# Attention on one core: rows of Q, K and V dealt to the partitions four in a row

## The chip, the cores and the metric

The kernel runs on one core of a Trainium2 chip. The metric is device time in microseconds of one execution, the median of three runs of the plain program. A profiled execution gives the trace; its times are those that the views below show. Engines are called by the profile's names: PE (TensorE, the matrix engine) and PEld (its weight loads), DVE (VectorE), ACT (ScalarE), POOL (GpSimd) and SP (SyncE, which here only issues transfers). Transfers run on 16 DMA engines that all queues share.

## The reference

```python
def setup_inputs():
    batch = 8
    seq_len = 2048
    d_model = 512
    # q, k, v: float32 [batch, seq_len, d_model]

def reference(q, k, v):
    d_k = q.shape[-1]
    scores = np.matmul(q, k.transpose(0, 2, 1)) / np.sqrt(d_k)
    attn_weights = special.softmax(scores, axis=-1).astype(np.float32)
    return np.matmul(attn_weights, v)
```

Eight independent attentions of 2048 queries on 2048 keys, without a mask. For one query the order of the keys doesn't matter, as long as K and V have the same one, and each query's output depends on no other query.

## The kernel before, in words

**Tiles.** A batch of K, Q or V is four chunks of 512 rows; a chunk is four tiles of 128 rows. With the old layout, row `p` of tile `n` stands on partition `p`, so a partition holds rows `p`, `128 + p`, `256 + p` and `384 + p` of the chunk (`srcs`, "(n p) d -> p n d"). All is computed in float16 with sums in float32.

**Loads.** `load` (line 118) brings a chunk of Q or K, 1 MB of float32, in one transfer of POOL's queue that casts to float16 on the way into a staging tile; there are three staging tiles (`stage`). `load_v` (line 207) brings a chunk of V straight into `vraw`, one of two buffers for a batch. In `vraw` two rows of V lie side by side, each with a gap of eight elements behind it (`VP = D + 8`); the gap behind the second one holds a 1, which makes the matmul sum the weights of the softmax as a 257th column. `dma_transpose` (line 143), on SP's queue, turns a staged chunk into `kops[c][0]` (`kraw`) or `qraw`, with the 512 dimensions on partitions, and frees the staging tile. `store` (line 405), on SP's queue too, writes a finished tile of 128 queries by 512 to memory. The output tiles come from a pool of seven (`opool`).

**Products.** Both products are done as two-by-two blocks with seven products in place of eight. For the scores, `Group` takes a pair of key tiles and 1024 queries (`sp`), for which DVE forms sums of blocks of K (`k_sums`, lines 181 to 184) and of Q (`q_sums`, lines 198 to 201); its matmuls stand on line 291. The exponential (line 227) leaves the weights in `left` and `right`, keys on partitions. For the output, `Pair` takes one tile of 128 queries from each half of the 1024 and all keys; DVE forms sums of the weights (`p_sums`, lines 340 to 343) and of V (`v_sums`, lines 215 to 218); its matmuls stand on line 386, with V's blocks as the moving operand of 256 or 257 columns. ACT and DVE scale and combine the results (lines 395, 398, 418 to 447), and `store` sends them off.

**Order.** The order of all work is written out by hand. The main loop runs over 32 steps `g`, four for a batch, each with 28 slots of score products of the coming 1024 queries between the output products of the present ones. `PLAN` says in which slot the next batch's chunks are loaded and transposed; `KSUMS`, `VSUMS` and `sums_of` say when DVE forms the sums. A load waits on POOL's queue for a free staging tile (that is, for an earlier transpose) or for the V buffer of two batches ago.

**The opening.** The first chunks of Q and K come row tile by row tile as float32, in eight transfers of 256 KB on the queues of SP and ACT (`load_first`, line 128), and are cast by DVE and ACT (`round_first`, line 132). Once the first tile of K has landed, POOL issues the other loads of batch 0 in the order `LOADS = 'q1 k1 q2 k2 k3 v0 v1 q3 v2 v3'`, `q1` in two pieces of two tiles; some land in `right` and `left` of the second set of weight tiles, which are not in use yet (`SPARE`), so the profile shows them as `right<-in_k_dram` and the like. PE itself transposes the chunks of Q and K of batch 0 (line 153), except `q2`, which SP's queue transposes. Then POOL waits twice, on lines 694 and 695, until that transpose and the last chunk of V have landed, before it issues loads for batch 1. Until the first rows are there, PE runs matmuls on zeros (`idle`, line 657).

Of the kernel before, what the change touches and what calls it, by code (L numbers as in the profile page):

```python
# [12 lines left out]
def kernel(  # L13
# [21 lines left out]
    nc = tc.nc  # L35
    P = 128
    B, T, D = q.shape
    F16 = mybir.dt.float16
# [11 lines left out]
    NT = QH // P  # L50
    NQT = 2 * NSP
    NJ = NKB // 2
    CH = 4
    NCH = NKB // CH
    H = D // 2
    VP = D + 8
    TP = H + 8
    NG = NJ // 2
    NE = 6
# [3 lines left out]
    const = ctx.enter_context(tc.tile_pool(name="const", bufs=1))  # L63
# [12 lines left out]
    def bank(name):  # L76
        t = psum[name].tile([P, 512], F32, tag=name)
        return t
# [10 lines left out]
    for c in range(NCH):  # L89
# [3 lines left out]
    qraw = [const.tile([P, 2 * NT, ND, P], F16, name=f"qraw{n}") for n in range(2)]  # L93
    qsum = [const.tile([P, NT, 2, P], F16, name=f"qs{n}") for n in (1, 2, 4)]

    vraw = [const.tile([P, NJ, 2, VP], F16, name=f"vh{n}") for n in range(2)]
    vt1 = const.tile([P, NJ, TP], F16, name="vt1")
    vt2 = const.tile([P, NJ, H], F16, name="vt2")
    vt4 = const.tile([P, NJ, H], F16, name="vt4")
# [1 line left out]
    pts = {}  # L101

    srcs = {
        "k": k.rearrange("b (n p) d -> b p n d", p=P),
        "q": q.rearrange("b (n p) d -> b p n d", p=P),
        "v": v.rearrange("b (n p) d -> b p n d", p=P),
    }

    def load(what, b, c, pieces=(CH,), room=None):
        t = staged.get((what, b, c))  # L110
        if room is not None:
            t = staged[what, b, c] = room
        if t is None:
            t = staged[what, b, c] = stage.tile([P, CH, D], F16, tag="stage", name="stage")
        n = CH - sum(pieces)
        for w in pieces:
            at = c * CH + n
            nc.gpsimd.dma_start(out=t[:, n:n + w, :], in_=srcs[what][b, :, at:at + w, :])
            n += w

    firsts = {}
# [1 line left out]
    def load_first(what, n, queue, room):  # L123

        if (what, 0, 0) not in staged:
            staged[what, 0, 0] = stage.tile([P, CH, D], F16, tag="stage", name="stage")
        firsts[what, n] = room
        queue.dma_start(out=room, in_=srcs[what][0, :, n, :])

    def round_first(what, n):  # L130
        f = nc.vector.tensor_copy if what == "q" else nc.scalar.copy
# [8 lines left out]
    def dma_transpose(what, b, c):  # L140
        src = staged.pop((what, b, c))
        dst = raw_of(what, b, c)
        nc.sync.dma_start_transpose(
            out=dst[:, 0:CH].rearrange("p n c r -> p (n c) r"),
            in_=src[:].rearrange("p n d -> p (n d)"),
        )
# [30 lines left out]
    def k_sums(c):  # L177
        a11, a12, a21, a22 = k_blocks(c)
        _, s1, s2, s4 = kops[c]
        return [  # L180
            lambda: add(s1[:], a21, a22),
            lambda: sub(a21, a11, a21),
            lambda: sub(s2[:], s1[:], a11),  # L183
            lambda: sub(s4[:], a12, s2[:]),
        ]
# [16 lines left out]
        ]  # L202

    def load_v(b, c):
        dst = vraw[b % 2][:].rearrange("p j s d -> p (j s) d")
        ns = slice(c * CH, (c + 1) * CH)
        nc.gpsimd.dma_start(out=dst[:, ns, 0:D], in_=srcs["v"][b, :, ns, :])

    def v_sums(b, c):
        vh = vraw[b % 2]  # L210
        js = slice(c * CH // 2, (c + 1) * CH // 2)
        b11, b12 = vh[:, js, 0, 0:H], vh[:, js, 0, H:D]
        b21, b22 = vh[:, js, 1, 0:H], vh[:, js, 1, H:D]
        return [
            lambda: sub(vt1[:, js, 0:H], b12, b11),
            lambda: sub(vt2[:, js], b22, vt1[:, js, 0:H]),
            lambda: sub(b12, b22, b12),
            lambda: sub(vt4[:, js], b21, vt2[:, js]),
        ]
# [39 lines left out]
    class Group:  # L259
# [6 lines left out]
        def product(self, n):  # L266
            c, j = divmod(self.j, 2)
            a11, a12, a21, a22 = k_blocks(c)
            b11, b12, b21, b22 = q_blocks(self.sp)
            _, s1, s2, s4 = kops[c]  # L270
            t1, t2, t4 = qsum
            t3 = t3_of(self.sp)
            if n == 1:
                if self.sp not in pts:
                    new_p(self.sp)
                self.left, self.right = pts[self.sp]
                self.x = bank("qx")
# [12 lines left out]
            for dc in range(2):  # L290
                nc.tensor.matmul(  # L291
                    dst[:], lhs[:, j, dc, :], rhs[:, :, dc, :],
                    start=(n in (1, 5) and dc == 0), stop=(dc == 1),
                    skip_group_check=True,
                )
            getattr(self, f"after{n}", lambda: None)()
# [49 lines left out]
    def columns(g, which):  # L346
        i = g % 2 * 2 + "ab".index(which)
        return slice(i * P, (i + 1) * P)

    class Pair:  # L350
# [6 lines left out]
        def product(self, n, j0=0, j1=NJ):  # L357
            g = self.g
            left, right = pts[g // 2]
            s1, s2, s4 = psums.get((g, self.which), (None,) * 3)  # L360
            vh, t1, t2, t4 = vraw[g // NQT % 2], vt1, vt2, vt4
            cols = columns(g, self.which)
            alone = g >= NP - 2 and self.which == "b"
            own = "q" if alone else "p"
            self.apart = g == NP - 1
            if n == 1 and j0 == 0:
                self.x = bank("px")
            elif n == 2:
                self.y = bank(own + "y")
            elif n == 5:  # L370
                self.z = bank(own + "z")
            lhs, rhs, dst = {
                1: (lambda j: left[0][:, j, cols], lambda j: vh[:, j, 0, 0:H], "x"),
                2: (lambda j: left[1][:, j, cols], lambda j: vh[:, j, 1, 0:H], "y"),
                3: (lambda j: s4[:, j, :], lambda j: vh[:, j, 1, H:D + 1], "z"),
                4: (lambda j: right[:, j, 1, cols], lambda j: t4[:, j, :], "x"),
                5: (lambda j: s1[:, j, :], lambda j: t1[:, j, 0:H + 1], "z"),
                6: (lambda j: s2[:, j, :], lambda j: t2[:, j, :], "x"),
                7: (lambda j: right[:, j, 0, cols], lambda j: vh[:, j, 0, H:D], "x"),
            }[n]  # L380
# [20 lines left out]

        def store(self, o, half, ds=slice(0, D), queue=nc.sync):
            b, sp = divmod(self.g // 2, NSP)
            n = (2 * sp + half) * NT + self.g % 2 * 2 + "ab".index(self.which)
            queue.dma_start(out=out[b, n * P:(n + 1) * P, ds], in_=o[:, ds])

        def store_first(self, ds):
            if self.apart:
# [88 lines left out]
    def prefetch(g, slot):  # L497
        b, qt = divmod(g, NQT)
        if (g, slot) == (0, 12):
            nc.gpsimd.memset(vraw[1][:, :, 1, D:D + 1], 1.0)  # L500
# [98 lines left out]
    nc.gpsimd.memset(vraw[0][:, :, 1, D:D + 1], 1.0)  # L599

    def row():
        t = opool.tile([P, D], F32, tag="o", name="first")
# [13 lines left out]
    gate = const.tile([P, 1], F32)  # L616
# [10 lines left out]
    for n, word in enumerate(LOADS.split()):  # L627
        what, c = word[0], int(word[1])
# [63 lines left out]
    dma_transpose("q", 0, 2)  # L692

    nc.gpsimd.tensor_copy(out=gate[:], in_=qraw[1][:, NT - 1, ND - 1, 0:1])
    nc.gpsimd.tensor_copy(out=gate[:], in_=vraw[0][:, NJ - 1, 1, D - 1:D])

    braid = []
    for n, (j, own, edges) in enumerate(FIRST_GROUPS):
# [75 lines left out]
```

## Time and profile before

| | |
|---|---|
| median of three runs | 802.04 us (801.6 to 802.36) |
| profiled execution | 800.94 us, of which the span in the trace is 799.2 us |
| granted TensorE clock | 1.00 |
| instructions | 14,622 |
| DMA packets | 188,870, with 115.80 MB written |
| HBM | 100.70 MB read, 33.55 MB written |

The span runs from the first to the last instruction in the trace. A packet is one run of bytes that a DMA engine moves; sizes are those written, so a load that casts from float32 to float16 reads twice as much. `q0` is POOL's queue, `q1` is SP's. The busy share of DMA engines can be over 100%, since packets of one engine overlap. In a list of groups the columns are line, engine, operation, output and inputs, size and count, then busy time and the mean of one. The groups of transfers (KB as written, median time from issue to landing):

```profile
out_dram<-o SPq DMA_DIRECT2D x124, 256.0 KB, 3.5
vh<-in_v_dram POOLq DMA_DIRECT2D x32, 512.0 KB, 10.5
stage<-in_k_dram POOLq DMA_DIRECT2D x29, 512.0 KB, 8.0
stage<-in_q_dram POOLq DMA_DIRECT2D x28, 512.0 KB, 7.9
right<-in_k_dram POOLq DMA_DIRECT2D x2, 512.0 KB, 13.2
...
right<-in_q_dram POOLq DMA_DIRECT2D x2, 256.0 KB, 5.3
right<-in_q_dram POOLq DMA_DIRECT2D x1, 512.0 KB, 10.4
left<-in_q_dram POOLq DMA_DIRECT2D x1, 512.0 KB, 22.8
qraw<-stage SPq DMA_TRANSPOSE x28, 6.3
kraw<-stage SPq DMA_TRANSPOSE x28, 7.2
```

These times hold the waiting in the queue: the ten loads of the opening are issued within ten microseconds and land over thirty.

### The profile page before, as it was taken

What the parts mean: (1) busy time and instruction counts of PE and PEld (TensorE: products, weight loads), DVE (VectorE), ACT (ScalarE), POOL (GpSimd) and SP (SyncE); (2) the same over time, 40 slices, a digit from 0 to 9 for tenths busy, and PEclk for the clock granted to TensorE, in tenths of its full rate; (3) what the DMA queues carried; (4) which work ended last, traced back from release to release, by engine and by line L of the source; (5) the groups of instructions that cost most, each with busy time, mean ns of one, the idle gap of its engine ahead of it and who ended that gap; (6) DMA issues with size and microseconds to landing.
All of it is one profiled execution on the core that took longest, in us unless ns stands there. A gap on an engine that the chain in (4) does not pass through costs nothing.

```text
span 799.2 us, 14622 instructions
## 1 busy us (share of the span) xinstructions
PE 793.7 (99%) x5556; PEld 538.1 (67%) x5556; DVE 557.6 (70%) x1230; ACT 572.0 (72%) x1020; POOL 71.5 (9%) x105
## 2 busy tenths in 40 slices
PE   9999999999999999999999999999999999999998
PEld 6566666666666666666666666666666666666677
DVE  5786767857677676866768667686776857678564
ACT  4877777777777767777777777777677777776752
POOL 4011110001101010010100110001110011000000
PEclk9999999999999999999999999999999999999999
DMA  9999992899828999399994999849993598711112
GB/s 222 175 176 177 207 172 73 156 183 196 166 60 156 182 197 145 80 161 178 177 158 78 173 177 186 128 93 155 203 217 86 96 205 160 162 40 41 44 52 104
DMA packets 188870, 115.80 MB, mean 145 GB/s; under 512 B 122496, under 2 KB 171904, under 8 KB 188800
## 3 DMA queue, kind: packets, MB, share of 16 engines
q0 software_dynamic: 49648, 49.29, 42.9%
q1 hardware_dynamic: 138576, 65.16, 38.3%
q8 instruction: 43, 0.70, 0.4%
q10 hardware_dynamic: 576, 0.43, 0.2%
q14 instruction: 27, 0.22, 0.1%
HBM read 100.70 MB, written 33.55 MB: 168 GB/s over the span
## 4 chain that ended last, share of the span: by engine, by line
PE 99%; DMA 0%; DVE 0%; ACT 0%; issue 0%
PE t L386 49%; PE t L291 46%; PE t L234 1%; PE t L250 1%; PE tr L153 1%; DMA first<-in_q_dram 0%; PE t L657 0%; DVE kraw L156 0%; ACT o L395 0%; DVE stage L132 0%; DVE o L447 0%
## 5 line engine op out<-in xcount | busy, mean ns | idle before, releaser
L291 PE MATMUL t<-qraw,kraw 128*128 128x512 f16 x732 | 198.1, 379 | 0.0
L395 ACT ACTIVATE o<-t,r 128x256 f32<-128x256 f32 (+1 forms) x256 | 121.1, 473 | 100.5 <-DVE r L418 69.5
L386 PEld LDWEIGHTS <-s 128*128 128x128 f16 x1536 | 150.3, 98 | 56.5
L227 ACT ACTIVATE left<-t 128x512 f16<-128x512 f32 x256 | 154.1, 603 | 37.0 <-PE t L291 30.8
L398 DVE SCALAR_TENSOR_TENSOR o<-t,r,o 128x256 f32<-128x256 f32 x192 | 92.4, 482 | 102.1 <-PE t L386 60.9
L291 PEld LDWEIGHTS <-kraw 128*128 128x128 f16 x984 | 96.2, 98 | 64.2 <-issue 0.3
L291 PE MATMUL t<-qs,ks 128*128 128x512 f16 x492 | 136.5, 379 | 0.0
L386 PE MATMUL t<-vh,left 128*128 128x256 f16 x1024 | 133.0, 273 | 0.0
L386 PE MATMUL t<-vt,s 128*128 128x257 f16 (+1 forms) x1024 | 133.0, 273 | 0.0
L227 ACT ACTIVATE right<-cz 128x1024 f16<-128x1024 f32 x123 | 130.5, 1061 | 1.1 <-DVE cz L311 1.1
L386 PEld LDWEIGHTS <-left 128*128 128x128 f16 x1024 | 100.2, 98 | 37.6
L386 PEld LDWEIGHTS <-right 128*128 128x128 f16 x1024 | 100.2, 98 | 37.5 <-issue 0.4
L305 ACT COPY cz<-t 128x512 f32<-128x512 f32 x122 | 71.4, 585 | 72.8 <-PE t L291 72.4
L311 DVE TENSOR_TENSOR cz<-t,cz 128x512 f32<-128x512 f32 x123 | 84.5, 687 | 52.8 <-PE t L291 52.7
L314 DVE TENSOR_TENSOR cz<-t,cz 128x512 f32<-128x512 f32 x123 | 84.9, 690 | 43.0 <-PE t L291 41.6
L291 PEld LDWEIGHTS <-ks 128*128 128x128 f16 x738 | 72.1, 98 | 48.3 <-DVE ks L183 0.3
L291 PE MATMUL t<-qraw,ks 128*128 128x512 f16 x246 | 73.2, 379 | 0.0
L291 PE MATMUL t<-qs,kraw 128*128 128x512 f16 x246 | 73.2, 379 | 0.0
L301 ACT COPY t<-t 128x512 f32<-128x512 f32 x121 | 69.0, 570 | 4.0 <-PE t L291 0.8
L308 ACT COPY cz<-t 128x512 f32<-128x512 f32 x123 | 71.5, 581 | 0.0
L386 PE MATMUL t<-vh,s 128*128 128x257 f16 x512 | 66.7, 273 | 0.0
L386 PE MATMUL t<-vh,right 128*128 128x256 f16 x512 | 66.2, 273 | 0.1
(62 smaller groups left out, 574.0 us busy)
## 6 DMA issues: line engine op xcount, KB each, us to landing
out_dram<-o SPq DMA_DIRECT2D x124, 256.0 KB, 3.5
vh<-in_v_dram POOLq DMA_DIRECT2D x32, 512.0 KB, 10.5
stage<-in_k_dram POOLq DMA_DIRECT2D x29, 512.0 KB, 8.0
stage<-in_q_dram POOLq DMA_DIRECT2D x28, 512.0 KB, 7.9
right<-in_k_dram POOLq DMA_DIRECT2D x2, 512.0 KB, 13.2
out_dram<-o SPq DMA_DIRECT2D x6, 128.0 KB, 1.7
first<-in_q_dram SPq DMA_DIRECT2D x2, 256.0 KB, 3.3
cz<-in_q_dram SPq DMA_DIRECT2D x2, 256.0 KB, 4.8
```

Of the source, the lines that this page charges most:

```text
L153: nc.tensor.transpose(tr[:, m, dc, :], src[:, n + m, dc * P:(dc + 1) * P], ident[:])
L227: nc.scalar.activation(out=out_, in_=in_, func=EXP, scale=inv_sqrt_d)
L234: nc.tensor.matmul(st[:], kops[c][0][:, n, dc, :], qraw[0][:, half * NT:(half + 1) * NT, dc, :], start=(dc == 0), stop=(dc == ND - 1),)
L291: nc.tensor.matmul(dst[:], lhs[:, j, dc, :], rhs[:, :, dc, :], start=(n in (1, 5) and dc == 0), stop=(dc == 1), skip_group_check=True,)
L301: self.edges[0](out=self.y[:], in_=self.x[:])
L305: self.edges[1](out=self.cz[:, 1, :], in_=self.z[:])
L308: nc.scalar.copy(out=self.cz[:, 0, :], in_=self.x[:])
L311: nc.vector.tensor_add(self.cz[:, 1, :], self.x[:], self.cz[:, 1, :])
L314: nc.vector.tensor_add(self.cz[:, 0, :], self.z[:], self.cz[:, 0, :])
L386: nc.tensor.matmul(dst[:, 0:width], lhs(j), rhs(j), start=(first and j == 0), stop=(j == NJ - 1), skip_group_check=True,)
L395: nc.scalar.activation(out=out_, in_=src, func=COPY, scale=r[:])
L398: nc.vector.scalar_tensor_tensor(out=out_, in0=src, scalar=r[:], in1=out_, op0=MULT, op1=ADD)
```

## The change

Within a chunk of 512 rows, partition `p` now holds rows `4p` to `4p + 3` ("(c p n) d -> c p (n d)"). What was tile `n` of a chunk, rows `128 n + p`, is now rows `4p + n`. Q, K and V have the same dealing, so the weights and the products are the same up to the order of keys and queries, and `store` writes tile `n` of a chunk to rows `4p + n`.

For the transfers: a chunk of Q or K is one run of 8 KB in memory for each partition instead of four of 2 KB. A chunk of V is two runs of 4 KB: in `vraw` the two rows of a pair now stand without a gap, and the 1 and its gap stand behind both, so each pair has 2 x 512 + 8 elements where it had 2 x 520. The two pieces of `q1` have one run of 4 KB each for a partition. The first eight row tiles and the stores still move runs of 2 KB, now 8 KB apart in memory; the pieces of the last stores move 512 or 1024 bytes, 8 KB apart. No instruction is added or taken out.

```diff
-    VP = D + 8
...
-    vraw = [const.tile([P, NJ, 2, VP], F16, name=f"vh{n}") for n in range(2)]
+    vraw = [const.tile([P, NJ, 2 * D + 8], F16, name=f"vh{n}") for n in range(2)]
...
     srcs = {
-        "k": k.rearrange("b (n p) d -> b p n d", p=P),
-        "q": q.rearrange("b (n p) d -> b p n d", p=P),
-        "v": v.rearrange("b (n p) d -> b p n d", p=P),
+        what: x.rearrange("b (c p n) d -> b c p (n d)", p=P, n=CH)
+        for what, x in (("k", k), ("q", q), ("v", v))
     }
+    outs = out.rearrange("b (c p n) d -> b c n p d", p=P, n=CH)
+
+    def flat(t):
+        return t[:].rearrange("p n d -> p (n d)")
...
         for w in pieces:
-            at = c * CH + n
-            nc.gpsimd.dma_start(out=t[:, n:n + w, :], in_=srcs[what][b, :, at:at + w, :])
+            nc.gpsimd.dma_start(
+                out=flat(t)[:, n * D:(n + w) * D],
+                in_=srcs[what][b, c, :, n * D:(n + w) * D],
+            )
             n += w
...
-        queue.dma_start(out=room, in_=srcs[what][0, :, n, :])
+        queue.dma_start(out=room, in_=srcs[what][0, 0, :, n * D:(n + 1) * D])
...
     def load_v(b, c):
-        dst = vraw[b % 2][:].rearrange("p j s d -> p (j s) d")
-        ns = slice(c * CH, (c + 1) * CH)
-        nc.gpsimd.dma_start(out=dst[:, ns, 0:D], in_=srcs["v"][b, :, ns, :])
+        js = slice(c * CH // 2, (c + 1) * CH // 2)
+        nc.gpsimd.dma_start(
+            out=vraw[b % 2][:, js, 0:2 * D],
+            in_=srcs["v"][b, c].rearrange("p (j e) -> p j e", e=2 * D),
+        )
...
-        b11, b12 = vh[:, js, 0, 0:H], vh[:, js, 0, H:D]
-        b21, b22 = vh[:, js, 1, 0:H], vh[:, js, 1, H:D]
+        b11, b12, b21, b22 = (vh[:, js, n * H:(n + 1) * H] for n in range(4))
...
-                3: (lambda j: s4[:, j, :], lambda j: vh[:, j, 1, H:D + 1], "z"),
+                3: (lambda j: s4[:, j, :], lambda j: vh[:, j, D + H:2 * D + 1], "z"),
...
-            n = (2 * sp + half) * NT + self.g % 2 * 2 + "ab".index(self.which)
-            queue.dma_start(out=out[b, n * P:(n + 1) * P, ds], in_=o[:, ds])
+            n = self.g % 2 * 2 + "ab".index(self.which)
+            queue.dma_start(out=outs[b, 2 * sp + half, n, :, ds], in_=o[:, ds])
```

The other changed lines give the same elements of V under their new addresses: products 1, 2 and 7 in `Pair`, the two memsets of the 1, and the gate on line 695.

More of the change, by code (lines that the diff above doesn't have):

```diff
@@ L372, in product @@
             lhs, rhs, dst = {
-                1: (lambda j: left[0][:, j, cols], lambda j: vh[:, j, 0, 0:H], "x"),
-                2: (lambda j: left[1][:, j, cols], lambda j: vh[:, j, 1, 0:H], "y"),
-                3: (lambda j: s4[:, j, :], lambda j: vh[:, j, 1, H:D + 1], "z"),
+                1: (lambda j: left[0][:, j, cols], lambda j: vh[:, j, 0:H], "x"),
+                2: (lambda j: left[1][:, j, cols], lambda j: vh[:, j, D:D + H], "y"),
+                3: (lambda j: s4[:, j, :], lambda j: vh[:, j, D + H:2 * D + 1], "z"),
                 4: (lambda j: right[:, j, 1, cols], lambda j: t4[:, j, :], "x"),
@@ L378, in product @@
                 6: (lambda j: s2[:, j, :], lambda j: t2[:, j, :], "x"),
-                7: (lambda j: right[:, j, 0, cols], lambda j: vh[:, j, 0, H:D], "x"),
+                7: (lambda j: right[:, j, 0, cols], lambda j: vh[:, j, H:D], "x"),
             }[n]
@@ L499, in prefetch @@
         if (g, slot) == (0, 12):
-            nc.gpsimd.memset(vraw[1][:, :, 1, D:D + 1], 1.0)
+            nc.gpsimd.memset(vraw[1][:, :, 2 * D:2 * D + 1], 1.0)
         for kind, what, c in PLAN.get((qt, slot), ()):
@@ L598 @@
     nc.gpsimd.memset(vt1[:, :, H:H + 1], 1.0)
-    nc.gpsimd.memset(vraw[0][:, :, 1, D:D + 1], 1.0)
+    nc.gpsimd.memset(vraw[0][:, :, 2 * D:2 * D + 1], 1.0)
     def row():
@@ L694 @@
     nc.gpsimd.tensor_copy(out=gate[:], in_=qraw[1][:, NT - 1, ND - 1, 0:1])
-    nc.gpsimd.tensor_copy(out=gate[:], in_=vraw[0][:, NJ - 1, 1, D - 1:D])
+    nc.gpsimd.tensor_copy(out=gate[:], in_=vraw[0][:, NJ - 1, 2 * D - 1:2 * D])
     braid = []
```

## The prediction

> **What bounds the kernel now.** I read the page first: busy time by engine, the queues, the chain of work that ended last.
>
> ```profile
> PE 793.7 (99%) x5556; PEld 538.1 (67%) x5556; DVE 557.6 (70%) x1230; ACT 572.0 (72%) x1020; POOL 71.5 (9%) x105
> ...
> q0 software_dynamic: 49648, 49.29, 42.9%
> q1 hardware_dynamic: 138576, 65.16, 38.3%
> ...
> PE 99%; DMA 0%; DVE 0%; ACT 0%; issue 0%
> ```
>
> TensorE is busy for all but 5.5 us of the span and owns 99% of the chain. The DMA engines are also busy for 81% of the time (42.9 + 38.3), yet no transfer holds more than the very first link of the chain (the first row of Q, 0.4%). A busy PE may still be a slow PE, so the next view is the windows: matmuls in equal stretches, in the columns PE, PEld, DVE, ACT, POOL, granted clock, DMA share, GB/s.
>
> ```profile
> 100.00:200.00 100.00, 100.00 (x692) 67.54 (x690) 71.31 (x158) 73.27 (x131) 9.11 (x13) 1.00 0.91 157
> 200.00:300.00 100.00, 100.00 (x692) 67.69 (x691) 70.88 (x157) 73.07 (x132) 9.99 (x14) 1.00 0.81 152
> 700.00:760.00 60.00, 60.00 (x415) 40.38 (x413) 41.80 (x93) 44.07 (x79) 0.00 (x0) 1.00 0.12 45
> 780.00:799.20 19.20, 15.58 (x142) 13.65 (x140) 9.15 (x22) 4.99 (x11) 0.00 (x0) 1.00 0.27 97
> ```
>
> The pace is 6.92 matmuls per us at a DMA share of 0.91, 6.92 at 0.81, and 415/60 = 6.92 again where all loads are over and the share is 0.12. So traffic on the DMA engines does not slow a matmul, and lighter traffic will not speed one up. What a load can do is come too late. The only place where PE lives close to its loads is the opening, so I asked who waited there, between 9 and 42 us (total, times, longest). PE itself waits for nobody; its weight loads do:
>
> ```profile
> PEld L250 <- DVE qraw L156: 0.4, 1, 0.4
> PEld L291 <- DVE ks L183: 0.3, 1, 0.3
> PEld L234 <- DVE kraw L156: 0.2, 1, 0.2
> PEld L153 <- DMA right<-in_k_dram: 0.2, 1, 0.2
> ```
>
> Four short waits, and they run ahead of the matmuls that they feed. One is for a load: chunk 2 of K, issued at 8.24 us, takes 12.2 us to land, that is until 20.4, and its transposes on PE begin at 20.49. So loads are just in time here: they can lose, they have nothing to win.
>
> **The change, part by part.** Instruction by instruction nothing moves. The order on PE, ACT, DVE, SP and POOL is the same in both programs, and so are the waits, but for one sum on DVE at about 60 us that names a further semaphore, of the first Q load, long landed. What changes is the shape of three kinds of transfer.
>
> (1) *The loads of POOL's queue, 1 MB of float32 each, cast on the way.* A chunk was 512 runs of 2 KB and becomes 128 runs of 8 KB (Q, K) or 256 of 4 KB (V). Two windows of the DMA view give the price of a packet before (packets, MB written, share of 16 engines): 16.5 to 21.5 us, where this queue is alone, and 22 to 29 us, where a transpose runs beside it.
>
> ```profile
> q0 software_dynamic: 1038, 1.03, 124.2%
> ...
> q0 software_dynamic: 1095, 1.09, 91.3%
> q1 hardware_dynamic: 1084, 0.28, 29.6%
> ```
>
> Alone, one engine starts a packet every 5 us x 16 / 1038 = 77 ns, and each takes 1.242 x 77 = 96 ns, so neighbours overlap. A chunk of 512 packets is 32 per engine, 2.47 us. No row shows an 8 KB cast packet, so bounds: if bytes set the pace it takes 4 x 77 = 308 ns and the chunk stays at 2.47 us; if the fixed part of a packet is saved (96 - 77 = 19 ns as the largest guess, three times in four) 251 ns and 2.0 us; if wide packets no longer overlap, 4 x 96 = 383 ns and 3.06 us. I take 2.47: the queue already reads 2 x 206 = 412 GB/s there, steadily, which looks like a limit in bytes. Earlier landings are worth 0 us, since PE's pace from 9 to 780 us has no gap that a load ends. Cover: the next landing in line is always ahead of its use, by 0.1 us (K chunk 2) to some 15 us (later batches). Without that cover every microsecond of lateness in the opening is a microsecond of PE.
>
> (2) *Sharing with SP's queue.* In the second window the queues alternate packet for packet: 1095 to 1084. A pair costs 7 us x 16 / 1090 = 103 ns, so a 256-byte packet of a transpose costs about 26 ns beside a load; alone, at 58 us, 562 of them in 0.5 us, 14 ns. With packets four times as long SP's transposes and stores get fewer turns while a load runs, and all of them once it has ended. The opening is again the tight place: the transpose of Q chunk 2 (2048 packets, 128 per engine) starts at about 21.5 us, with five loads still queued.
>
> ```profile
> 36.79 0.25 POOL L694 CAST gate<-qraw 128x1 f32<-128x1 f16 x1 [20.97 <-DMA qraw<-right]
> ...
> 37.64 0.69 DVE L198 TENSOR_TENSOR qs<-qraw 128x1024 f16<-128x1024 f16 x1
> ```
>
> It lands just before 36.79, where POOL's gate sees it; the first sum that reads it begins at 37.64. After: five loads are 5 x 2.47 = 12.4 us and, with V's four at 16 packets per engine and Q's at 8, 72 turns for the transpose, 72 x 26 ns = 1.9 us; the other 56 packets follow alone in 56 x 14 ns = 0.8 us. 21.5 + 12.4 + 1.9 + 0.8 = 36.6 us: about as before. The work is the same and something always has the engines; only the order changes. Cost 0 us.
>
> Later batches have more room. The first chunk of K for batch 1 is transposed from 58.06 us and first read at 75.38, 17.3 us later, while such transposes land in 4.3 to 12.6 us:
>
> ```profile
> 58.06 2.19 SPq L143 DMA_TRANSPOSE kraw<-stage  x1
> ...
> 75.38 0.42 DVE L181 TENSOR_TENSOR ks<-kraw 128x512 f16<-128x512 f16 x1
> ...
> DMA to landing us min/median/max: 4.3/7.2/12.6
> ```
>
> A store (8 packets per engine) beside a load may land 8 x (308 - 77) ns = 1.9 us later; behind it stands a pool of seven output tiles, four of which are used up in some 24 us. 0 us.
>
> (3) *The first eight rows and all stores: 2 KB runs as before, now 8 KB apart in memory.* Alone the row loads start a packet every 83 ns (270 of them in the 1.4 us from 6.0). No row shows what the distance does. Bounds: nothing, or as dear as the worst stretch of POOL's queue, 8.2 to 8.9 us, 16 x 0.7 us / 125 = 90 ns. That is 16 packets x 7 ns = 0.1 us for the first rows of Q and K, which stand on the chain; below nothing by the same 0.1. The last stores, 1.6 us to landing, have two to four packets per engine: under 0.1 us. I take 0.
>
> (4) *V without the gap between its two rows, and the ones moved behind both.* The same matmuls of 256 or 257 columns and the same sums on other addresses. The first row of each pair (`vh` with `right`) and the second (`vh` with `s`) start at different offsets today and both take 273 ns on the page. 0 us.
>
> Sum: 0. The profiled execution has a span of 799.2 us in 800.94; the three plain runs have a median of 802.04. I forecast 799.2 and 802.0. The forecast's own range, from the bounds in (3) and a microsecond of slip in (2), is 801.2 to 803.4.
>
> **The rivals.**
>
> *Wide packets lose their overlap (slower).* Place: POOL's queue in the opening. For it: today 24% of a packet's time is hidden behind its neighbour, and nothing shows that an 8 KB cast is split as finely. Against it: bytes, not packets, look like the limit. Price: 0.6 us per load. K chunk 2 is the fourth load, 2.4 us late against a margin of 0.1; Q chunk 3 is the eighth, 4.8 us late against 0.6 (it lands at 34.1, its transposes load at 34.73). PE is stopped for 4.2 us in all: 806.2. It decides as soon as a chunk takes over about 2.7 us.
>
> *Transposes starved (slower).* For it: the alternation one for one. Against it: the sum in (2). If SP's queue gets even less than its turn, the transpose of Q chunk 2 ends only after V's last chunk, for which POOL's second gate opens at 39.7, plus 0.8: 40.5 where 37.64 is due, and DVE has 0.3 us of idle time from there to 42.5. PE would lose some 2.5 us: 804.5. The Trainium skill, in "DMA: Bandwidth & Descriptors", section "Queues, rings and completion order", says that each engine goes round the queues that have work and changes only between packets; the counts 1095 and 1084 agree. Taken alone that rule speaks against this change, as the queue with the wider packets gets the larger share; by it the time would be anything between my forecast and this rival's 804.5.
>
> *The runs stay short.* If descriptors are cut back to 2 KB, everything lands as before: 802.0, with some 49,600 packets on the queue of POOL.
>
> *Faster.* It would need matmuls that run faster with less descriptor traffic: 1 ns each is 5.6 us, 796.5. The three windows above speak against it. Earlier loads alone cannot do it: the idle time of PE is 5.5 us, of which some 3.6 lie after the last matmul.
>
> **How the numbers follow.** Forecast 0.60 and short runs 0.04 (both no change), lost overlap 0.14, starved transposes 0.10, faster 0.07, and 0.05 for a slip at the first rows or the stores that is larger than its bounds. About 0.2%, 1.6 us, is what can be told from no change here. So faster 0.07, same 0.64, slower 0.29. The predicted time is the forecast's, 802.0. The range goes up to 806.3, to take in both slower rivals, and down to 800.6; it leaves out about 0.13.
>
> **What would show it.** POOL's queue falls from 49,648 packets to about 18,000 (61 x 128 + 256 for Q and K, 32 x 256 for V, and the 1,520 small ones that 94 x 512 leaves of today's count). Its share of the engines stays near 40%. Matmuls stay at 692 per 100 us, and between 9 and 42 us PE's weight loads wait no longer than now. The gate on Q chunk 2 opens within a microsecond of 36.8, the transposes of K stay under 14 us to landing. The forecast is wrong if PE shows idle time in the opening (lost overlap: behind loads of K or Q; starved transposes: behind DVE's sum on Q), or if the pace of the matmuls moves at all.

## The result: 1.9 us slower, and the profile after

| | before | after |
|---|---|---|
| median of 11 runs each, same chip | 802.07 us (800.6 to 802.82) | 803.94 us (802.11 to 804.89) |
| ratio, 95% interval | | 1.0023 [1.0014, 1.0033] |
| profiled execution | 800.94 us, span 799.2 us | 804.89 us, span 803.1 us |

The change costs 1.9 us. The profiled execution after is the longest of its 11 runs and the one before is near the short end of its own, so the two profiles lie 3.9 us apart (803.1 - 799.2): the traces show the loss enlarged. A second profile of the changed kernel has a span of 802.5 us.

The page of the changed kernel, the lines that answer to those shown of before:

```profile
PE 795.7 (99%) x5556; PEld 539.3 (67%) x5556; DVE 557.2 (69%) x1230; ACT 572.5 (71%) x1020; POOL 58.4 (7%) x105
...
q1 hardware_dynamic: 138576, 65.16, 39.1%
q0 software_dynamic: 17776, 49.29, 38.7%
...
PE 94%; DMA 5%; DVE 0%; ACT 0%; POOL 0%; issue 0%; ACTq 0%; DVEq 0%
```

POOL's queue went from 49,648 to 17,776 packets, so the runs did become long. (The trace counts 14,623 instructions against 14,622: one semaphore instruction on DVE is new, all others are the same in number.) The chain of work is the new thing: DMA held none of it to speak of, now it holds 5%. The windows of the changed kernel (PE, PEld, DVE, ACT, POOL, granted clock, DMA share, GB/s) tell where this is not:

```profile
100.00:200.00 100.00, 100.00 (x693) 67.46 (x691) 70.39 (x155) 73.39 (x132) 7.13 (x12) 1.00 0.91 149
200.00:300.00 100.00, 100.00 (x692) 67.58 (x691) 71.15 (x158) 73.14 (x132) 7.12 (x12) 1.00 0.82 156
700.00:760.00 60.00, 60.00 (x416) 40.59 (x415) 41.72 (x92) 43.90 (x79) 0.00 (x0) 1.00 0.12 45
```

The pace is the same 692 matmuls per 100 us. The loss is older than 100 us. The chain in order of time, cut to the first 50 us of the changed kernel (start, us, what), gives its place:

```profile
1.12 5.37 DMA first<-in_k_dram
...
6.54 0.19 POOL gate L622
...
8.39 11.29 DMA right<-in_q_dram
...
19.69 21.68 DMA qraw<-right
...
41.46 0.70 DVE qs L202
```

Read it downwards: the first row of K lands at 6.49 us and opens POOL's gate; POOL issues the load of Q chunk 2, which lands at 19.68; SP's queue transposes it, until 41.37; then DVE forms the sum on it. PE has no part in the chain up to there. The same steps before, in the timeline of POOL and of SP's queue (start, us, instruction, in brackets what it waited for):

```profile
5.12 0.18 POOL L617 COPY gate<-first 128x1 f32<-128x1 f32 x1 [4.22 <-DMA first<-in_k_dram]
...
17.92 7.06 SPq L143 DMA_TRANSPOSE qraw<-right  x1
```

So the gate opens 1.4 us later, the transpose is issued 1.8 us later (19.69 against 17.92), and it is 2.9 us longer in flight, as the DMA views of before and then of the changed kernel have it:

```profile
qraw<-right SPq DMA_TRANSPOSE x1, 18.7
...
qraw<-right SPq DMA_TRANSPOSE x1, 21.7
```

It lands 4.7 us later. Before, POOL's gate saw it at 36.79 and DVE's sum on it began at 37.64, so it had some 0.8 us to spare. Now the sum begins at 41.46, 3.8 us later, and the spans lie 3.9 us apart.

PE falls behind in the opening in another way too, which this chain hides. The view by tile shows it in the first full tiles, `qraw` by `kraw` on 128 x 512 (shortest, median and longest in ns, first and last in us), before and then after:

```profile
L234 PE MATMUL t<-qraw,kraw x48: 379/379/389, 17.2 to 38.6; 128*128 128x512 f16 x48
```

```profile
L239 PE MATMUL t<-qraw,kraw x48: 379/379/389, 20.0 to 41.5; 128*128 128x512 f16 x48
```

2.8 us are gone before 20 us. 1.5 of them are lost by the first product of Q and K (9.19 us against 7.67), in waits of PE for DVE's casts of the first rows, as DVE itself waits for the DMA. The other 1.3 go by while PE's clock is still low, of which more below: from 9 to 13 us PE is busy all the time in both profiles, with 52 matmuls before and 39 after.

### The profile page after: what moved, and what is told of

Read it like the earlier page. It is cut to its first block, busy times and chain, and to the rows that moved or that the text cites. A ratio compares the mean times of both kernels' runs of the same rounds, so it can differ in the third digit from the quotient of the medians.

```text
span 803.1 us, 14623 instructions
## 1 busy us (share of the span) xinstructions
PE 795.7 (99%) x5556; PEld 539.3 (67%) x5556; DVE 557.2 (69%) x1230; ACT 572.5 (71%) x1020; POOL 58.4 (7%) x105
## 3 DMA queue, kind: packets, MB, share of 16 engines
q0 software_dynamic: 17776, 49.29, 38.7%
## 4 chain that ended last, share of the span: by engine, by line
PE 94%; DMA 5%; DVE 0%; ACT 0%; POOL 0%; issue 0%; ACTq 0%; DVEq 0%
PE t L391 49%; PE t L296 45%; DMA qraw<-right 3%; DMA right<-in_q_dram 1%; DMA first<-in_k_dram 1%; POOL right L119 0%; ACT right L232 0%; ACT o L400 0%; DVE qs L202 0%; DVE cz L316 0%; DVE qraw L204 0%; POOL stage L119 0%; ACT left L232 0%; ACT cz L313 0%; DVE vt L221 0%
## 5 line engine op out<-in xcount | busy, mean ns | idle before, releaser
L391 PE MATMUL t<-vt,right 128*128 128x256 f16 x512 | 66.3, 273 | 0.0
```

The source lines that it names most:

```text
L391: nc.tensor.matmul(dst[:, 0:width], lhs(j), rhs(j), start=(first and j == 0), stop=(j == NJ - 1), skip_group_check=True,)
```

## Two things that can end last in the opening

Set side by side, the profiles of all kernels follow one reading. Let *start* be the first matmul of those tiles and *gate* the moment when POOL's gate on Q chunk 2 opens, just after its transpose has landed. Before has start 17.2 and span 799.2, so what follows a start takes 782.0 us; the changed kernel has gate 41.51 and span 803.1, so what follows a late gate takes 761.6. The span should be the larger of start + 782.0 and gate + 761.6. The other rows were not used for the two constants. Times in us; the edits are told in the next section. The ratio and its interval are worked out over all runs and are not the quotient of two medians: for rows_new the ratio means 1.7 us where the medians differ by 1.1.

| kernel | start | gate | start + 782.0 | gate + 761.6 | span | median of runs | ratio to before, same chip |
|---|---|---|---|---|---|---|---|
| before | 17.2 | 36.79 | **799.2** | 798.4 | 799.2 | 802.07 | |
| after | 20.0 | 41.51 | 802.0 | **803.1** | 803.1 | 803.94 | 1.0023 [1.0014, 1.0033] |
| again | 19.8 | 40.92 | 801.8 | **802.5** | 802.5 | 803.75 | 1.0028 [1.0018, 1.0039] |
| late_wide | 18.1 | 36.99 | **800.1** | 798.6 | 800.1 | 801.61 | 1.0003 [0.9994, 1.0012] |
| rows_new | 18.2 | 38.18 | **800.2** | 799.8 | 800.3 | 802.55 | 1.0021 [1.0012, 1.003] |
| rows_new2 | 18.3 | 38.53 | **800.3** | 800.1 | 800.8 | 802.69 | 1.0024 [1.0015, 1.0032] |
| open_wide | 17.7 | 41.25 | 799.7 | **802.9** | 802.6 | 803.66 | 1.0028 [1.0017, 1.0039] |
| open_held | 18.1 | 36.18 | **800.1** | 797.8 | 801.5 | 802.40 | 1.0019 [1.001, 1.0028] |
| rows_old | 18.2 | 40.40 | 800.2 | **802.0** | 802.1 | 804.94 | 1.0049 [1.0035, 1.0062] |
| rows_old2 | 16.9 | 39.73 | 798.9 | **801.3** | 801.4 | 805.59 | 1.0053 [1.0038, 1.0069] |
| held | 19.4 | 34.50 | **801.4** | 796.1 | 801.6 | 803.66 | 1.0029 [1.0019, 1.0039] |
| fixed | 17.1 | 33.30 | **799.1** | 794.9 | 799.5 | 802.67 | 1.0024 [1.0005, 1.0043] |
| dummies | 18.5 | 40.11 | 800.5 | **801.7** | 801.7 | 804.11 | 1.0034 [1.0022, 1.0047] |
| split | 17.6 | 39.46 | 799.6 | **801.1** | 801.2 | 804.26 | 1.0032 [1.002, 1.0044] |
| two_rows | 18.0 | 39.40 | 800.0 | **801.0** | 801.0 | 802.92 | 1.0021 [1.0012, 1.003] |
| warm | 17.0 | 36.65 | **799.0** | 798.3 | 799.0 | 801.11 | 1.0001 [0.9993, 1.001] |
| rows_new_warm | 21.8 | 40.87 | **803.8** | 802.5 | 804.9 | 802.42 | 1.0018 [1.0009, 1.0028] |

Of the 15 rows that set no constant, 13 come within 0.5 us. The two others, open_held (+1.4) and rows_new_warm (+1.1), have a third wait that their traces name (below).

The chain that the profile traces bears this choice out in most rows, not in all. It runs through the transpose in after, open_wide, rows_old, rows_old2 and dummies, as the sums say. In again, split and two_rows, where the gate's sum is also the larger, it runs along PE from the first rows until 41 or 42 us and then over DVE. In these three DVE's sum on Q chunk 2 waits 0.6 to 1.4 us for the transpose, and DVE has no gap for 5 us from there; that the late transpose sets their end through this backlog is argued from the timeline and not shown by the chain. In rows_new, rows_new2 and rows_new_warm the chain runs through POOL's gate on the first row of K and a load of K behind it.

What the wide packets do to the transpose shows most directly in its time in flight, from issue to landing. It is 18.6 to 19.1 us in the six kernels whose opening has no wide packet (before, warm, late_wide, rows_new, rows_new2, rows_new_warm), 20.7 to 22.9 in the eight that have some, and 15.5 to 18.5 in the three that have some but hold V's last chunks back (held, fixed, open_held).

The reading of the table was made after the runs, not forecast. It holds for single executions: a start also depends on when the clock of PE rises, which differs from one execution to the next, so medians are compared only with their intervals.

It explains why the parts of the loss do not add. Two delays run side by side, and mending one uncovers the other.

## The experiments

All variants compute the same as the reference; what differs is which rows a partition holds, and when a load is issued.

**rows_new and rows_new2: the long distance alone.** The kernel before, with the new dealing for chunk 0 of batch 0 only. Its rows lie 8 KB apart; no load of Q or K gets longer runs.

```diff
+    def dealt(b, c):
+        return (b, c) == (0, 0)
...
-        queue.dma_start(out=room, in_=srcs[what][0, :, n, :])
+        src = news[what][0, 0, :, n, :] if dealt(0, 0) else srcs[what][0, :, n, :]
+        queue.dma_start(out=room, in_=src)
```

> The kernel before, with the new dealing for chunk 0 of batch 0 alone: its eight first row loads (and V's chunk 0, and that chunk's stores) read 2 KB runs 8 KB apart; every other transfer as before, no packet is wider. Theory A (the late first rows and the clock that rises later): the first row of Q lands at 4.2 to 4.6 us instead of 3.7, K's at 6.0 to 6.6 instead of 5.1, TensorE's clock rises after 9 us instead of at 7.1, and the time is 1.0 to 2.0 us over before (803.1 to 804.1). Theory B (the wide packets of POOL's queue starve SP's transposes): no difference, 802.1. Theory C (wide packets in later batches): 802.1.

Measured: 802.55 against 801.43 us, slower by 1.1; with the interval, by 1.0 to 2.4. The clock rose at 4.5 us and not after 9. The same kernel a second time:

> The kernel before with the new dealing for chunk 0 of batch 0 alone, repeated as the partner of the next: 0.8 to 2.0 us over before.

Measured: 802.69 against 801.03, slower by 1.7. The transposes of PE in the timeline of the first of these runs:

```profile
4.81 0.40 PE L166 MATMUL tr<-ident,stage 128*128 128x128 f16 x4 [0.88 <-DVE stage L145]
...
7.11 0.40 PE L166 MATMUL tr<-ident,stage 128*128 128x128 f16 x4 [1.47 <-DVE stage L145]
```

They begin at 4.23 and 5.69 us before. Here PE waits 0.88 and 1.47 us for casts whose rows have landed late. The chain of the same run, cut to its first steps (start, us, what), goes another way, over the first row of K and the load of K's chunk 1 that stands behind POOL's gate on that row:

```profile
1.13 5.07 DMA first<-in_k_dram
...
6.26 0.18 POOL gate L634
...
7.90 8.45 DMA stage<-in_k_dram
...
16.39 1.07 PE tr L166 x16
```

Before, that gate opened at 5.12 us. So the late rows are felt in two places: by PE, and by all loads that POOL issues behind the gate. The queues between 2 and 5 us (packets, MB, share of 16 engines), of before and then of the changed kernel, show the transfers themselves:

```profile
q1 hardware_dynamic: 395, 0.73, 65.2%
q10 hardware_dynamic: 244, 0.28, 26.2%
```

```profile
q1 hardware_dynamic: 198, 0.37, 45.2%
q10 hardware_dynamic: 182, 0.22, 43.5%
```

On SP's queue half as many packets move in the same 3 us, and each takes longer: 3 x 16 x 0.452 / 198 = 110 ns against 3 x 16 x 0.652 / 395 = 79 (ACT's queue, q10, holds other small packets too). rows_new has 199 packets at a share of 48.9% there, as the changed kernel. That the distance of the rows costs a microsecond or more is shown (V's chunk 0 and the stores of that chunk are dealt anew here too, but no wait of PE names them). Why, is not.

**late_wide: wide runs from batch 1 on.** The kernel before with `return b > 0` in the lines above.

> The kernel before, with the new dealing from batch 1 on (Q and K in runs of 8 KB, V still in runs of 2 KB because its gaps are kept; stores 8 KB apart); the opening is the one of before. Theories A and B: nothing on TensorE's path changes, 802.1. Theory C: most of the loss, 803.5 to 804.

Measured: 801.61 against 801.43, no difference, with an interval from 0.5 us under to 1.0 us over. So no cost of the wide runs of Q and K, nor of the stores, is seen behind the opening; V's wide runs are not in this kernel. Nor do 8 KB runs win anything later, though a chunk of K now takes 6.3 us from issue to landing instead of 8.0 (medians).

**rows_old and rows_old2: wide runs, rows in time.** The changed kernel with chunk 0 of batch 0 dealt as before, in its loads and stores (V's chunk 0 in two transfers).

```diff
-        queue.dma_start(out=room, in_=srcs[what][0, 0, :, n * D:(n + 1) * D])
+        queue.dma_start(out=room, in_=olds[what][0, 0, n])
```

> The changed kernel, with the old dealing for chunk 0 of batch 0 alone (V's chunk 0 then comes in two transfers of 256 KB); all other loads keep the wide runs. Theory A: the first rows land as before (3.7 and 5.1 us), the clock rises at about 7, and most of the loss is gone: 802.1 to 802.9, the rest being the wait for the transpose of Q chunk 2. Theory B: the transpose of Q chunk 2 still lands 3 us or more after it is due and the time stays at 803.5 to 804. Theory C: 803.9.

Measured: 804.94 against 801.43, slower by 3.5, so worse than the change itself and than any of the three theories gave.

> The changed kernel with the old dealing for chunk 0 of batch 0, repeated beside the changed kernel. Theories A and B together: the transpose still lands at about 40 us and sets the time, so undoing the rows alone gains nothing: within 0.8 us of the changed kernel, with a longer wait of DVE (1.5 us or more). If the rows were the whole loss: 1.5 us or more below it. If splitting V's chunk 0 into two transfers is what made this kernel slow: over 1 us above it.

Measured: 805.59 against 801.57, over 802.91 to 810.5. That is 1.8 us above the changed kernel on the same chip (next run), the outcome that pointed to the split of V's chunk 0. The rows land as before, the start is back at 16.9, and the end is set by the transpose: its gate opens at 39.73, and DVE waits 2.3 us for it. That the rows were a cost, and not the only one, agrees with the table. The runs up to 810.5 do not: none of these was caught in a profile.

**again:** the changed kernel once more, for a second profile.

> The changed kernel once more, for a second profile and for times on the same chip as the next three. Theory A (late first rows) and theory B (wide packets hold up the transpose of Q chunk 2), now taken together: both delays push the same chain, the rows at its start and the transpose at about 41 us, so they overlap and do not add up. 1.5 to 3 us over before; the transpose lands between 39.5 and 41.5 us and DVE's first sum on Q chunk 2 waits 0.5 to 1.5 us for it.

Measured: 803.75 against 801.57. The gate opens at 40.92, and DVE's sum waits 0.6 us for the transpose. The chain that ends last is another one than in the first profile: it runs from the first rows of Q along PE until 42.15 us and then over DVE. So in this execution the two delays nearly coincide (801.8 and 802.5 in the table).

**dummies:** the changed kernel with three more matmuls on zeros at each of two waits for rows.

```diff
-    idle(5)
+    idle(8)
...
-    idle(2)
+    idle(5)
```

> The changed kernel with three more matmuls on zeros before the first transposes (eight for five) and three more before the second ones (five for two), which fill the waits for the first rows of Q. Theory A with the clock as a part of the loss: the clock rises before 9 us instead of at 12.5, and the time falls by 0.6 to 1.3 us against the changed kernel, to 802.6 to 803.3, although the rows land as late as they do there. If the lateness alone counts and not the clock: 803.9 or up to 0.5 more.

Measured: 804.11 against 801.43, no gain, as for lateness alone. In its profile the clock rose at 7.2 us instead of 12.5, and the start came at 18.5 instead of 20.0; but the gate at 40.11 ends last, so that an earlier PE is worth nothing here.

**held: the transpose helped, rows late.** The changed kernel with V's chunks 2 and 3 issued only behind the gate on Q chunk 2, so that fewer loads share the engines with its transpose.

```diff
         if what == "v":
-            load_v(0, c)
+            if c < 2:
+                load_v(0, c)
...
+    for c in (2, 3):
+        load_v(0, c)
```

> The changed kernel with V's chunks 2 and 3 of batch 0 issued behind POOL's wait for the transpose of Q chunk 2 instead of ahead of it, so that fewer wide packets stand beside the transpose. Theory B: the transpose lands before 37 us, DVE's wait for it and the gaps on TensorE between 41 and 48 us are gone, and the time falls by 0.8 to 1.7 us against the changed kernel; what is left over before (0.8 to 2 us) is the first rows. If the transpose were not what TensorE waits for: no change.

Measured: 803.66 against 801.57; the median did not move from that of *again*, where a fall of 0.8 us or more was expected. Its gate, in the timeline:

```profile
34.50 0.18 POOL L700 CAST gate<-qraw 128x1 f32<-128x1 f16 x1 [22.09 <-DMA qraw<-right]
```

The transpose is 6.4 us earlier than in *again* and off the path, and PE is busy for 9.99 of the 10 us from 40, against 9.47 after. But the start at 19.4 is left, and 782.0 behind it is 801.4. The edit did to the transpose what it should, and the other delay took its place.

**fixed: both at once** (held and rows_old).

> Both: the old dealing for chunk 0 of batch 0, and V's chunks 2 and 3 behind POOL's wait; all other loads wide. Theories A and B together: both parts of the loss are gone, within 0.6 us of before. If there is a third part (V's chunk 0 in two transfers, stores 8 KB apart, wide packets in later batches): 1 us or more over before.

Measured: 802.67 against 801.57, so 1.1 us over before: not within 0.6, but what was expected if there is a third part. The profiled execution has start 17.1 and a span of 799.5, as before the change, and 800.46 is its shortest run; but its runs reach 810.38. So both delays can be undone together, as single executions show, and something that no profile caught keeps the median up. The median is 2.9 us under that of rows_old2, where holding V back moved nothing when the rows were late, as the larger of two delays would have it; but the intervals of these two kernels (0.4 to 3.4 and 3.0 to 5.5 us over before) overlap. The scatter stays.

**split: is it V's chunk 0 in two transfers that scatters?** The changed kernel with that alone.

> The changed kernel with V's chunk 0 of batch 0 in two transfers of one pair each (runs of 4 KB, new dealing), nothing else. It asks why the kernels with the old dealing for chunk 0 scatter from 803 to 810 us. Theory S (the split, which shifts the later loads of POOL's queue and what they wait for): this kernel scatters too, and its median is over 805. Theory E (wide packets that start early, beside rows that come in time): it stays with the changed kernel, 803.3 to 804.3, no run over 805.5.

Measured: 804.26 against 801.4, over 802.98 to 805.34 in five runs. Neither the median over 805 nor the scatter came, so nothing speaks for the split. Five runs do not rule it out: the five of rows_old, which has the split, lie just as close (803.89 to 805.79).

**two_rows: a smaller distance.** Chunk 0 of batch 0 dealt two rows to a partition: 4 KB apart.

> The changed kernel with chunk 0 of batch 0 dealt two rows in a row: its row loads read 2 KB runs 4 KB apart, V's chunk 0 stays one transfer with runs of 4 KB, all else is wide. If the distance of the first rows costs by the stretch of memory that they touch: the first rows of Q and K land between those of before and of the changed kernel (3.7 to 4.4 and 5.1 to 6.2 us), and the time lies 0.5 to 1 us under the changed kernel. If only contiguous rows are quick: as the changed kernel. Theory S expects no scatter here, theory E some (up to 806).

Measured: 802.92 against 801.4, which is neither outcome as told. The first two rows land as before (casts at 3.76 and 5.28 us), yet the third row of Q is late: cast at 8.72, before at 7.53. The delay moved one step on and did not go away; start 18.0.

**open_wide: wide runs of Q and K in the opening alone.** The kernel before with `return b == 0 and c > 0`.

> The kernel before, with the new dealing for chunks 1 to 3 of batch 0 alone: Q and K of the opening in runs of 8 KB, V still in runs of 2 KB, chunk 0 and all later batches as before; no transfer is split. If wide packets of Q and K hold up the transpose of Q chunk 2: it lands after 38 us, DVE waits, 0.5 us or more over before. If it is V's packets that do it, or the split: within 0.4 us of before. Theory E: scatter and 2 us or more over before.

Measured: 803.66 against 801.4, slower by 2.3, with all first rows in time. The waits between 33 and 50 us (total, times, longest):

```profile
DVE qs L211 <- DMA qraw<-right: 2.8, 1, 2.8
...
DVE vt L229 <- DMA vh<-in_v_dram: 1.6, 1, 1.6
...
PE t L305 <- DVE cz L328: 1.0, 1, 1.0
PE t L305 <- DMA qraw<-right: 0.9, 1, 0.9
```

DVE's sum on Q chunk 2 waits 2.8 us for the transpose, and PE stands behind it. Wide packets of Q and K alone produce the late transpose, which is 22.9 us in flight instead of 18.7; V's need not be wide. The 12 runs lie between 801.40 and 805.71, so the scatter of theory E is there too, though not up to 810.

**open_held:** open_wide with V's chunks 2 and 3 held back.

> The kernel before with the wide runs of Q and K in the opening (as in the run with wide packets in the opening alone), and V's chunks 2 and 3 of batch 0 behind POOL's wait for the transpose of Q chunk 2. No first row is late and nothing is split. If the wide packets cost by holding up that transpose: it lands before 36 us, the gaps on TensorE from 39 to 48 us are gone, and 1.2 us or more of the 2.3 us over before come back. If they cost in another way (late loads of K, V or Q chunk 3): 1.5 us or more over before remain, with gaps from 13 to 37 us.

Measured: 802.40 against 801.03; still slower by 1.4, so 0.9 us came back and not 1.2. The transpose is in time (36.18), and now the chunks of V that were held back are late:

```profile
DVE vt L229 <- DMA vh<-in_v_dram: 2.7, 2, 2.1
...
PE t L400 <- DMA vh<-in_v_dram: 0.9, 1, 0.9
```

That is the third wait, which the table does not know.

**warm and rows_new_warm: is part of it the clock?** The kernel before with one more matmul on zeros at each wait, and rows_new with three more.

> The kernel before with one more matmul on zeros ahead of each of the first two transposes (six for five, three for two), which close its two gaps of 0.3 and 0.4 us there. If gaps put off the rise of the clock: it rises at or before 7 us, 0.2 to 0.6 us under before. If not: equal, or 0.2 us over.

> The same with six more matmuls on zeros (eight for five, five for two) that fill TensorE's waits for the first rows. No wide packet, so no transpose sets the time as it did in the first run with more zeros. If a clock that rises late is a part of what the late rows cost: the clock rises before 9 us, and the time is 0.4 to 1.0 us under its partner. If only the lateness of the rows counts: equal to the partner within 0.3 us, or up to 0.5 us over it.

Measured: warm 801.11 against 801.03, rows_new_warm 802.42 against 802.69 of rows_new2: nothing beyond the uncertainty, and not the 0.4 us or more of a clock that counts. The profiled execution of rows_new_warm happened to be the longest of its 12 (806.65), and shows how a late load can cost more than its lateness. Windows (columns as above):

```profile
17.00:20.50 3.50, 1.09 (x19) 1.08 (x19) 0.00 (x0) 0.43 (x1) 0.74 (x1) 1.00 1.24 206
20.50:24.00 3.50, 3.50 (x15) 1.90 (x14) 2.32 (x4) 2.07 (x4) 0.00 (x0) 0.51 1.24 206
```

PE stops for 2.4 us for a chunk of K, which POOL's gate let go late (7.64 us, against 6.49 in rows_new2), and then runs at a granted clock of 0.51 for 3.5 us: 15 matmuls where open_wide has 27 in the same window. The runs of rows_old2 and fixed near 810 may come about like this; no profile of one shows it.

No version beats the kernel before.

## Why the prediction failed, step by step

The forecast was no change, 802.0; it is slower by 1.9. The range held the time. Two terms that the sum put at nothing failed: the end of the transpose in step (2) and the first rows in step (3).

*What bounds the kernel, and "can lose, nothing to win": right.* Matmuls kept their pace, and late_wide shows that earlier loads are worth nothing.

*Step (1), the price of a wide packet: right.* From 16 to 22 us, where POOL's queue is alone in the changed kernel:

```profile
DMA packets 343, 1.28 MB, mean 213 GB/s; under 512 B 34, under 2 KB 34, under 8 KB 342
...
q0 software_dynamic: 342, 1.26, 105.5%
```

343 - 1 - 34 = 308 wide packets, and 6 us x 16 / 308 = 312 ns: the 308 that was taken, not the 251 of a saving nor the 383 of lost overlap. Most of the overlap did go, from a share of 124.2% to 105.5%; but a wide packet takes at most 1.055 x 312 = 329 ns and not four times 96. That rival is out, and so is the one that the runs stay short.

*Step (2), the transpose of Q chunk 2: wrong in its last term.* The alternation holds. From 24 to 28 us, and then from 37 to 41.37, in the changed kernel:

```profile
q0 software_dynamic: 375, 0.74, 96.8%
q1 hardware_dynamic: 369, 0.09, 17.4%
...
q1 hardware_dynamic: 1058, 0.26, 87.5%
q0 software_dynamic: 99, 0.17, 20.4%
```

375 packets to 369: one for one. The Trainium skill ("DMA: Bandwidth & Descriptors", section "Queues, rings and completion order") says that an engine takes turns between its queues packet by packet; the trace agrees in the count. (The page's packet is a group of descriptors, the trace's is one run of bytes, so the counts do not show how long a turn is.) The turns last until 37 us (92 packets to 86 from 36 us on). I had put the end of the sharing at 35.8 for a transpose that is issued 1.8 us earlier than this one, with 56 packets per engine left; 1058 / 16 = 66 were left. So the length of the sharing and the count were near. The price was not: "56 x 14 ns = 0.8 us". From 37 to 41.37, with only 99 packets of POOL's queue beside it, the rest takes 4.4 us, 66 ns a packet on average. The 14 ns came from transposes at 58 us and did not hold here; why the average is so much higher is only in part seen (last section). The transpose landed at 41.37 and not at 36.6, with 37.64 due; 1.8 us of that come from its later issue, for which the late first row of K stands at the head of the chain, 2.9 from here. The gate was to open within 1 us of 36.8; it opened at 41.51.

*Step (3), the first rows 8 KB apart: wrong.* The bound was 0.1 us; alone they cost 1.1 and 1.7 (rows_new, rows_new2). The upper bound came from a stretch of another queue, which does not move this pattern, so it bounded nothing. A packet of these rows took 79 ns before and takes 110. I also saw only PE behind these rows, and not POOL's gate on the first row of K, behind which all other loads of the opening stand: they moved by 1.4 us as well.

*Step (4), V's layout:* not tried by itself. The pace after 100 us leaves no sign of a cost; late_wide keeps the old layout of V and says nothing about it.

*The rivals.* "Starved transposes" named the place, the mechanism and nearly the time (40.5 for the landing, 804.5). It had 0.10 because I trusted the sum in (2). The nearness of its time is in part luck: the rival knew nothing of the late rows, behind which the transpose was issued at 19.69 instead of 17.92. That rival's own end, V's last chunk plus 0.8 us, would have the same flaw, since it too took the tail at 14 ns. A slip at the first rows, which got 0.05, was the other half.

*The signs to look for.* Packets on POOL's queue, its share, the pace and the transposes of K (6.9 us median, 9.8 at most) came as said. PE's weight loads from 9 to 42 us wait no longer than before, and this said nothing: PE had lost its time ahead of 9 us and to a low clock after it, and for the transpose it was DVE that waited.

*Open.* Why the rows slow down with distance, what holds the transfers up at the end of a transpose, what scatters rows_old2 and fixed and keeps the median of fixed 1.1 us over before, and what part the clock has in the medians.

## What to carry to other kernels

Where the matmul engine has no gap that a load ends, longer runs won nothing, and the opening, where loads land just in time, was the only place where they were seen to matter: there, keep the first rows contiguous and the packets beside a just-in-time transfer short, and widen later loads if at all. Bound an access pattern that the trace doesn't show by a run of that pattern or leave the bound wide, and price the end of a transfer from the stretch it will end in, not from a quiet one. When two delays run side by side, an experiment that mends one may show nothing: read the span against both before calling a cause dead.

## What the hardware showed that was not expected

*A DMA transpose goes in bursts and stops.* In *held* the transpose has the engines nearly to itself from 30 us. Its queue from 31.5 to 32 us, from 32 to 32.5, from 32.5 to 33.5 and from 33.5 to 34:

```profile
q1 hardware_dynamic: 536, 0.14, 121.5%
...
q1 hardware_dynamic: 184, 0.05, 430.1%
...
q1 hardware_dynamic: 26, 0.01, 6.2%
...
q1 hardware_dynamic: 144, 0.03, 30.2%
```

First an engine starts a packet every 15 ns, close to the 14 of the prediction. The 184 of the next half microsecond take 4.301 x 0.5 us x 16 / 184 = 187 ns each on average (the share counts a packet where it starts, so they last beyond this window), and then only 26 start in a whole microsecond. The last 144 are quick again. Such a stop is in the opening of before as well, where it hits both queues: from 30 to 31 us 52 packets of SP's queue and 55 of POOL's start, in the next microsecond 157 and 155. In the changed kernel 91 packets of SP's queue start between 39 and 40 us, and 390 from there to the end. So the end of a transpose is not dear at an even rate, and no price per packet would have told it. In *held* and in before an instruction load (one packet of queue q8) starts in the window just ahead of the stop; whether it has to do with it was not tried.

*The clock of PE rises when it will.* Four transposes take 0.61 to 0.63 us at first and 0.39 later. In the changed kernel's timeline the step is here:

```profile
11.72 0.63 PE L157 MATMUL tr<-ident,stage 128*128 128x128 f16 x4
...
12.79 0.39 PE L157 MATMUL tr<-ident,stage 128*128 128x128 f16 x4
```

Before, it was between 6.52 and 7.91 us. In each trace the record of a granted clock of 1.00 begins at this step (12.53 us in the changed kernel, 7.14 before); ahead of it there is no record, and the windows show 1.00 there all the same. Over the 17 profiles it begins between 4.3 and 12.5 us. With the first rows late, a rise at 4.5 goes with a start at 18.2 and 18.3 (rows_new, rows_new2), at 12.5 with 20.0 and 19.8 (after, again), so it can be worth up to 1.8 us of start; the two pairs differ in the wide loads too. Nothing shows that the change moves it. The Trainium skill ("TensorE: Matmul & The Clock Gate", "Part 1: The HAM clock gate") gives some 4 us into sustained matmuls, give or take 0.5 us; here, where PE pauses for its rows, the spread is 8 us.
